# Down projection of a SwiGLU layer: where the gate and the residual are applied, and which engine adds the groups' sums

## The chip, the cores and the metric

The kernel runs on one core of a Trainium2 chip. The metric is the device time of one execution in microseconds. Engines are named as in the profile: PE is TensorE (matmul; PEld its weight load), DVE is VectorE, ACT is ScalarE, POOL is GpSimd, SP is the sync engine, whose queue issues the DMAs here.

## The reference

One inference step of a layer with 2048 features and 640 tokens (512 of the sample, 128 of the prompt): modulation, a mixer of attention and a recurrent scan, an output projection with residual and layer norm, then a SwiGLU layer with residual and a second layer norm. The change lies in the SwiGLU's last product and what stands behind it:

```python
def _post_norm(x, gate, f, g, b):
    return _layer_norm(ALPHA * x + gate * f, g, b)

def _swiglu(h, p):
    return (jax.nn.silu(h @ p["w_ffn_gate"]) * (h @ p["w_ffn_up"])) @ p["w_ffn_down"]

...
    x = _post_norm(x, g2, _swiglu(x * (1 + sc2) + sh2, p), p["ln2_g"], p["ln2_b"])
```

All inputs and outputs are float32. The gate g2 is one number per feature, another for the sample's tokens than for the prompt's. The kernel divides the whole by ALPHA, which the norm allows.

## The kernel before

Features lie on the 128 partitions, tokens along the free axis, in two halves `H1` and `H2` of 320 (the second half holds 192 tokens of the sample and 128 of the prompt). A float32 product is made of three products of float32r parts: weights are split into `qh` (cast on ACT) and `ql` (remainder, subtracted on DVE), operands likewise into a part and a remainder (tiles `p`, `t`).

The down projection has 22 pairs of contraction tiles in four groups c = 0 to 3 of 4, 6, 6 and 6 pairs. For each group, `operands` loads the pairs from `h_d` (tiles `hd`), forms Winograd's sums of them (POOL) and splits them (ACT casts, DVE remainders): per pair four POOL additions and, on DVE, one remainder `p` of 320 columns, one `p` of 640 and two `t` of 640. Then 8 pairs of feature tiles j follow, each one call of `strassen`: seven products in the order 1, 7, 5, 6, 2, 3, 4, each into a PSUM bank `b`. This is a set below. Sums of weights are formed on POOL and DVE (tiles `raw`). `strassen` copies product 1 to SBUF (`u1`, ACT), forms `u2` and `u3` on DVE and hands each of the four blocks of the result to `out(m, n, ps, u)`, as a bank and an SBUF tile to be added. In group c=3 products 2 and 4 are left out at first (the blocks of the first half of the tokens then have no bank, only `u1` and `u3`), and `rest` makes them behind all eight sets, so that the second half's norm can begin.

`out` is `gated`: DVE adds bank and tile to a tile `c` (L226), and multiplies by the gate and adds to the running result `z1` (L235), one instruction for a block of the first half and two, of 192 and 128 columns, for one of the second. `z1` begins as the residual: in group c=0 each of its 16 tiles is loaded from `z_d` (L1617) and gets the first norm's affine part on ACT (L238).

In c=3, `norms[1].add` takes each finished tile into the running sums of the layer norm, `nd` and `ns` on DVE, `nq` on ACT, `ns` on POOL. Behind the last group come the norms' ends and the output.

The order of each engine's instructions is set by a scheduler from the program's dependences and the tile pools' rooms: 8 small buffers of 320 columns (tag "ev": `c`, `u1` to `u3`, `nd`, `nq`), a pool of 640-column slots for `hd`, `p`, `t` and `z`, a few slots for weights. Each engine, SP's DMA queue too, then works in order.

Of the kernel before, what the change touches and what calls it, by code (L numbers as in the profile page):

```python
# [27 lines left out]
C = 64  # L28
# [40 lines left out]
# how long (us) the operands of a job's next products should take, beside the input projection and beside the attention  # L69
# [26 lines left out]
class Tensor:  # L96
    """TensorE, with a clock of the columns it has been given (us)"""
# [26 lines left out]
class Jobs:  # L124
    """The order of TensorE's work: of the jobs (generators) that are ready, the one of lowest rank goes on. A job yields the
    time until its next operands should be there, or a job to wait for"""
# [31 lines left out]
def step_kernel(ctx: ExitStack, tc: tile.TileContext, a: dict, o: dict, upto: int = 99, npairs: int = NPAIR, dbg=None):  # L158
# [81 lines left out]
    # ---- derived per-feature vectors  # L240
# [12 lines left out]
    # ---- weights: load, split in two float32r parts  # L253
# [19 lines left out]
    def mm3(ps, w, cols, x, first, last):  # L273
        """ps[128, 2, 0:320] += w.T @ x, both in two float32r parts"""
        (wh, wl), (xh, xl) = w, x
        for i, (ww, xx) in enumerate(((wh, xh), (wh, xl), (wl, xh))):
            for h in range(2):
                T.matmul(ps[:, h, :HN], ww[:, cols: cols + P], xx[:, h * HN: h * HN + HN],
                         start=first and i == 0, stop=last and i == 2)
            yield 0.0  # L280
# [6 lines left out]
    class Weights:  # L287
        """granules [128, 4 * 128] of weights in the order of use, each loaded and split while the one before is used"""
# [13 lines left out]
    def big(ps, ws, xs):  # L302
        """one feature tile"""
# [16 lines left out]
    # ---- adaLN  # L320
# [3 lines left out]
    def wmod_first(n, c0, w):  # L324
        """w columns from c0 on, in the room of what comes later"""
# [16 lines left out]
    def wmod_chunk(n, raws, c0=0, w=512):  # L342
        # in each group of 32 columns, the first two count
# [35 lines left out]
    # ---- input projection  # L379
# [22 lines left out]
    def token_shift(p0, p1, mi, mk=edge):  # L402
        """the tile's tokens (in two halves) shifted and mixed: 512 columns, one to skip, 128 columns"""
# [16 lines left out]
    # while w_mod streams in: the first feature tiles, two of them summed in PSUM, the others in SBUF  # L420
# [25 lines left out]
    def low_rank():  # L446
        """the decay's and the learning rate's low-rank inputs: leading parts twice along the partitions, remainders below
        each other"""
# [67 lines left out]
    def squares(j, t):  # L516
        """sums of squares of the queries' (4 tiles) and the keys' and values' (2 tiles) low-rank input, by token"""
# [13 lines left out]
    # ---- RWKV-7 heads, two at a time  # L531
# [9 lines left out]
    def hrow(h):  # L541
        """where head h keeps what pairs with its own features along the contraction"""
        return rows(1 - h)

    def wide(name):
        """[128, 10 chunks, 2, 64] in two slots' worth of memory"""
# [10 lines left out]
    def inverse(mab):  # L557
        """U = (I - N)^-1 for the strictly upper N of each chunk and head. Diagonal blocks of 16 in DVE's lanes, a block
        to a partition: (head, half) by (chunk of 16, block of 2), by substitution for 8 and one doubling; then two
        doublings on TensorE. Only the part of mab above the diagonal is used"""  # L560
# [18 lines left out]
        # the two blocks of 8 together  # L579
# [65 lines left out]
    def stat_cols(sq, rhs, n, bank=mps):  # L645
        """per 128 tokens: sum over the partitions of sq against rhs [128, n]; [128 tok, 5 * n] in PSUM"""
# [5 lines left out]
    def spread(st, n, ps2=None):  # L652
        """[128 tok, 5 * n] to [128, 640] feature-major, each of n columns on 128/n partitions: two PSUM tiles"""
# [22 lines left out]
    def nat(d, j):  # L676
        """tokens of half j of direction d, in natural order (read backward for d = 1)"""
# [7 lines left out]
    def rwkv_load(i):  # L685
        sh = {"carry": rtile("cy", 2 * C, "cy", 1)}
        raw = load_raw(a["lora"][i])
        # [leading parts; remainders] for the decay, [remainders; leading parts] for the learning rate
# [22 lines left out]
    def rwkv_decays(i, j, sh):  # L711
        """of the chunks of half j, in the order in which each direction reads them: decays within the chunk, keys"""
# [1213 lines left out]
```

## Time and profile before

| | |
|---|---|
| three runs | 3610.99, 3615.95, 3622.03 us; median 3615.95 |
| profiled execution, span | 3610.9 us |
| PE / DVE / ACT / POOL busy | 94% / 73% / 40% / 27% |
| down projection's first products | about 2934 us |
| c=1, c=2, c=3 begin | about 3057, 3230, 3405 us |

The stages ahead of the down projection take the first 2930 us. The profiled execution is one execution; its times are read against its own span. The starts of the groups are found by counting matmuls (672, 1008, 1008 and 1008 per group).

### The profile page before, as it was taken

The page shows a single profiled execution, that of the slowest core. Times are in us where ns is not written, and L with a number is a line of the kernel's source. Part 1 is how long each engine was busy: PE and PEld are TensorE (multiplying, and loading weights), DVE is VectorE, ACT ScalarE, POOL GpSimd, SP SyncE. Part 2 cuts the span into 40 slices and gives each one's busy share as a digit, 9 for nine tenths or more (in the row PEclk, how much of TensorE's full clock was granted, in tenths as well). Part 3 has the DMA queues.
Part 4 walks back from the last instruction along what each step waited for, and adds up shares of the span by engine and source line. Part 5 has one row for each costly group of instructions (what it writes and reads, how often), then busy time and mean ns, then how long its engine had stood idle before and what let it go on. Part 6 is the DMA issues. An engine that isn't in the chain of part 4 may idle for free. (4 is left out here: it accounts for less than half of the span.)

```text
span 3610.9 us, 70535 instructions
## 1 busy us (share of the span) xinstructions
PE 3388.5 (94%) x27538; PEld 3030.8 (84%) x27538; DVE 2625.3 (73%) x4729; ACT 1445.9 (40%) x2947; POOL 981.6 (27%) x944
## 2 busy tenths in 40 slices
PE   8979999999998999999979999999999988989887
PEld 4667777777886778799979999999999988989786
DVE  1455766676667777536998777777777799898998
ACT  1143433333343444423553444334444354444434
POOL 0021111120111222101374323333323353242545
PEclk9988999999998999999989999999999999999898
DMA  8653444444112111167534333333333343332333
GB/s 296 231 173 127 147 146 138 155 149 131 59 57 87 33 42 39 33 188 243 152 105 141 91 106 100 97 105 98 93 104 102 112 174 94 88 101 86 102 104 109
DMA packets 243054, 427.53 MB, mean 118 GB/s; under 512 B 25824, under 2 KB 76448, under 8 KB 242720
## 3 DMA queue, kind: packets, MB, share of 16 engines
q1 hardware_dynamic: 242720, 423.02, 37.1%
q8 instruction: 216, 3.54, 0.4%
q14 instruction: 118, 0.97, 0.1%
HBM read 374.73 MB, written 46.56 MB: 117 GB/s over the span
## 5 line engine op out<-in xcount | busy, mean ns | idle before, releaser
L226 DVE TENSOR_TENSOR ql<-raw,qh 128x512 fp32r<-128x512 f32 (+1 forms) x1072 | 870.7, 822 | 283.2 <-ACT qh L1325 277.0
L1325 ACT CAST qh<-raw 128x512 fp32r<-128x512 f32 (+1 forms) x1072 | 623.9, 586 | 928.9 <-PE b L112 782.9
L112 PE MATMUL b<-t,qh 128*128 128x320 f32 x4224 | 946.4, 313 | 18.2 <-ACT qh L1325 10.9
L112 PEld LDWEIGHTS b<-t,qh 128*128 128x128 f32 x4224 | 718.1, 191 | 23.5 <-ACT qh L1325 14.6
L112 PE MATMUL b<-p,qh 128*128 128x320 f32 x3168 | 713.0, 313 | 4.8 <-ACT qh L1325 3.3
L112 PE MATMUL b<-t,ql 128*128 128x320 f32 x2112 | 657.9, 315 | 32.3 <-DVE ql L226 32.0
L226 POOL TENSOR_TENSOR raw<-raw,raw 128x512 f32<-128x512 f32 (+1 forms) x288 | 390.4, 1357 | 862.4 <-DVE ql L226 664.7
L112 PEld LDWEIGHTS b<-p,qh 128*128 128x128 f32 x3168 | 538.5, 191 | 7.6 <-ACT qh L1325 5.2
L112 PE MATMUL b<-p,ql 128*128 128x320 f32 x1584 | 499.2, 315 | 36.1 <-DVE ql L226 35.7
L112 PEld LDWEIGHTS b<-t,ql 128*128 128x128 f32 x2112 | 401.8, 191 | 41.9 <-DVE ql L226 41.4
L112 PEld LDWEIGHTS b<-p,ql 128*128 128x128 f32 x1584 | 302.5, 191 | 45.7 <-DVE ql L226 45.6
L112 PE MATMUL acc<-xh,whi 128*128 128x320 f32 x1184 | 296.6, 333 | 6.2 <-ACT xh L269 5.9
L112 PE MATMUL acc<-xl,whi 128*128 128x320 f32 x1184 | 294.5, 331 | 0.0
L112 PE MATMUL acc<-xh,wlo 128*128 128x320 f32 x1184 | 292.6, 329 | 0.8 <-DVE wlo L226 0.8
L263 ACT CAST whi<-raw 128x512 fp32r<-128x512 f32 (+1 forms) x188 | 114.7, 610 | 340.1 <-PE acc L112 251.5
L226 DVE TENSOR_TENSOR wlo<-raw,whi 128x512 fp32r<-128x512 f32 (+1 forms) x188 | 129.3, 688 | 145.9 <-ACT whi L263 110.3
L112 PEld LDWEIGHTS acc<-xh,whi 128*128 128x128 f32 x1184 | 200.9, 195 | 34.4 <-issue 15.8
L226 DVE TENSOR_TENSOR raw<-raw,raw 128x512 f32<-128x512 f32 (+1 forms) x288 | 220.4, 777 | 8.8 <-POOL raw L226 6.3
L112 PEld LDWEIGHTS acc<-xh,wlo 128*128 128x128 f32 x1184 | 200.8, 195 | 22.2 <-issue 13.8
L112 PEld LDWEIGHTS acc<-xl,whi 128*128 128x128 f32 x1184 | 201.2, 195 | 19.3 <-issue 10.7
L112 PE MATMUL x<-wm,cs 128*32 128x512 f32 x768 | 140.3, 646 | 18.7 <-DMA wm<-in_w_mod_dram 18.2
L226 POOL TENSOR_TENSOR s<-s,c 128x320 f32<-128x320 f32 x88 | 104.6, 1189 | 138.6 <-DVE c L226 138.6
(329 smaller groups left out, 5134.4 us busy)
## 6 DMA issues: line engine op xcount, KB each, us to landing
wm<-in_w_mod_dram SPq DMA_DIRECT2D x64, 1024.0 KB, 5.4
raw<-in_w_gate_dram SPq DMA_DIRECT2D x188, 256.0 KB, 2.7
raw<-in_w_up_dram SPq DMA_DIRECT2D x188, 256.0 KB, 2.8
raw<-in_w_down_dram SPq DMA_DIRECT2D x224, 192.0 KB, 2.4
raw<-in_w_in_dram SPq DMA_DIRECT2D x132, 256.0 KB, 2.7
wm<-in_w_mod_dram SPq DMA_DIRECT2D x64, 512.0 KB, 6.2
raw<-in_w_out_dram SPq DMA_DIRECT2D x96, 256.0 KB, 3.1
hd<-s SPq DMA_DIRECT2D x44, 320.0 KB, 2.9
```

The source lines that it names most:

```text
L112: self.eng.matmul(out, lhsT, rhs, start=start, stop=stop)
L226: eng.tensor_tensor(out=out, in0=x, in1=y, op=op)
L263: A.copy(hi, r)
L1325: A.copy(hi, x)
```

## The change

For c < 3, `out` becomes `summed`: the blocks are added up without the gate. In c=0 DVE writes bank plus tile straight to `z1`, whose 16 tiles are now only rooms, taken ahead of the loop. In c=1 and c=2 POOL adds the SBUF tile to `z1`, then DVE adds the bank. For c=3, `gated` does the same POOL addition, DVE adds the bank if there is one, and then DVE multiplies by the gate and adds the residual. The residual is loaded there, per block of 320 columns, into a small buffer `zr` of the "ev" pool (`residual`, with the ACT instruction for the affine part). `rest` multiplies its bank by the gate and adds to `z1`, as before.

In numbers: 144 gate instructions on DVE go (six in each of 24 sets of c=0 to 2); 96 POOL additions of 128x320 come (64 in c=1 and 2, 32 in c=3); 16 loads of 320 KB and 16 ACT instructions on 640 columns in c=0 go, 32 loads of 160 KB and 32 ACT instructions on 320 columns in c=3 come. The products are the same. The rest of the diff removes comments.

```diff
-    def gated(kind, f, zz):
-        """z += gate * C"""
+    def summed(zz, first):
         def out(m, n, ps, u):
-            c = u if ps is None else ps if u is None else tmp("c")
-            if c is not ps and c is not u:
-                tt(V, c, ps, u, ALU.add)
+            z = zz[m][:, (H1, H2)[n]]
+            if first:
+                tt(V, z, ps, u, ALU.add)
+            else:
+                tt(G, z, z, u, ALU.add)
+                tt(V, z, ps, z, ALU.add)
+        return out
+    def gated(kind, f, zz, res):
+        def out(m, n, ps, u):
+            if u is not None:
+                z = zz[m][:, (H1, H2)[n]]
+                tt(G, z, z, u, ALU.add)
+                r = res(f + m, n)
+                if ps is not None:
+                    tt(V, z, ps, z, ALU.add)
             for o_, w, cnd in ((0, 192, 0), (192, 128, 1)) if n else ((0, HN, 0),):
                 z = zz[m][:, n * HN + o_: n * HN + o_ + w]
-                stt(z, c[:, o_: o_ + w], mcol(kind, f + m, cnd), z, ALU.mult, ALU.add)
+                g = mcol(kind, f + m, cnd)
+                if u is None:
+                    stt(z, ps[:, o_: o_ + w], g, z, ALU.mult, ALU.add)
+                else:
+                    stt(z, z, g, r[:, o_: o_ + w], ALU.mult, ALU.add)
         return out
...
-    # with the last of the contraction tiles, the second half of the tokens first
-    z1 = []
+    def residual(f, n):
+        r = tmp("zr")
+        DMA.dma_start(out=r, in_=z_d[f][:, (H1, H2)[n]])
+        act(r, r, AF.Identity, bias=vcol("ln1b", f), scale=vcol("ln1g", f))
+        return r
+    z1 = [fslot("z") for _ in range(KT)]
     k0 = 0
     for c, (npr, ng) in enumerate(((4, 1), (6, 2), (6, 2), (6, 2))):
         ops = operands(npr, lambda i: [loaded(h_d[2 * (k0 + i) + m], "hd") for m in range(2)], G)
         k0 += npr
         for j in range(8):
-            if c == 0:
-                for f in (2 * j, 2 * j + 1):
-                    z1.append(loaded(z_d[f], "z"))
-                    act(z1[f], z1[f], AF.Identity, bias=vcol("ln1b", f), scale=vcol("ln1g", f))
-            strassen(qs, ops, ng, gated(5, 2 * j, z1[2 * j: 2 * j + 2]), whole=c < 3)
+            zz = z1[2 * j: 2 * j + 2]
+            strassen(qs, ops, ng, summed(zz, c == 0) if c < 3 else gated(5, 2 * j, zz, residual), whole=c < 3)
             if c == 3 and j:
                 for z in z1[2 * j: 2 * j + 2] if j > 1 else z1[:4]:
                     norms[1].add(z)
...
             order = ExitStack()
             order.enter_context(tc.manual_schedule(engines={mybir.EngineType.PE}))
             for j in range(8):
-                rest(qs, ops, ng, gated(5, 2 * j, z1[2 * j: 2 * j + 2]))
+                rest(qs, ops, ng, gated(5, 2 * j, z1[2 * j: 2 * j + 2], None))
```

The first place is SP's queue while c=0 runs: `hd_5958` and the tiles behind it (before) and `hd_5926` and those behind it (after) are the operands of c=1's first pairs, `in_w_down4` are the weights of c=0, `in_w_down` those of c=1. Before:

```order
L1617 DMA z_5920_33430<-zd15_18068 128x640
L1617 DMA hd_5958_33593<-hd8_18017 128x640
L1617 DMA hd_5959_33595<-hd9_18018 128x640
L1387 DMA raw_5751_32659<-in_w_down4_dram 128x512
L1617 DMA hd_5960_33597<-hd10_18019 128x640
L1617 DMA hd_5961_33599<-hd11_18020 128x640
L1387 DMA raw_5755_32679<-in_w_down4_dram 128x512
L1387 DMA raw_5759_32698<-in_w_down4_dram 128x512
L1387 DMA raw_5766_32726<-in_w_down4_dram 128x512
L1617 DMA hd_5965_33610<-hd12_18021 128x640
```

After:

```order
L1387 DMA raw_5883_33273<-in_w_down4_dram 128x512
L1387 DMA raw_5898_33352<-in_w_down_dram 128x384
L1387 DMA raw_5899_33354<-in_w_down_dram 128x384
L1387 DMA raw_5903_33374<-in_w_down_dram 128x384
L1387 DMA raw_5904_33376<-in_w_down_dram 128x384
L1387 DMA raw_5908_33395<-in_w_down_dram 128x384
L1387 DMA raw_5909_33397<-in_w_down_dram 128x384
L1387 DMA raw_5915_33422<-in_w_down_dram 128x384
L1387 DMA raw_5916_33424<-in_w_down_dram 128x384
L1635 DMA hd_5926_33481<-hd8_18017 128x640
L1635 DMA hd_5927_33483<-hd9_18018 128x640
L1635 DMA hd_5928_33485<-hd10_18019 128x640
```

c=1's operands stood behind the residual's loads, among c=0's first weights; they now stand behind the last weights of c=0 and the first eight of c=1.

The second place is DVE, where the first of these operands are split. Before, this is the first third of c=0:

```order
L235 SCALAR_TENSOR_TENSOR z_5709_32473<-c_5734_32585,mod_90,z_5709_32473 128x320
L226 TENSOR_TENSOR p1_5962_33601<-hd_5958_33593,p1_5962_33601 128x320
L226 TENSOR_TENSOR c_5743_32629<-b_5740_32611,u3_5728_32558 128x320
L226 TENSOR_TENSOR ql_5742_32614<-raw_5716_32500,qh_5741_32613 128x512
L235 SCALAR_TENSOR_TENSOR z_5709_32473<-c_5739_32607,mod_90,z_5709_32473 128x192
L235 SCALAR_TENSOR_TENSOR z_5709_32473<-c_5739_32607,mod_90,z_5709_32473 128x128
L226 TENSOR_TENSOR p2_5964_33603<-hd_5959_33595,p2_5963_33602 128x640
L226 TENSOR_TENSOR ql_5748_32641<-raw_5720_32520,qh_5747_32640 128x512
L226 TENSOR_TENSOR ql_5753_32662<-raw_5724_32539,qh_5752_32661 128x512
L235 SCALAR_TENSOR_TENSOR z_5710_32476<-c_5743_32629,mod_90,z_5710_32476 128x320
```

After, it is c=0's end (`z_5653` is the last feature tile, `b_5922` its last product):

```order
L226 TENSOR_TENSOR z_5653_32237<-b_5922_33461,u3_5913_33416 128x320
L226 TENSOR_TENSOR ql_5983_33623<-raw_5981_33620,qh_5982_33622 128x384
L226 TENSOR_TENSOR p2_5932_33491<-hd_5927_33483,p2_5931_33490 128x640
L226 TENSOR_TENSOR p1_5935_33502<-hd_5928_33485,p1_5935_33502 128x320
L226 TENSOR_TENSOR p2_5937_33504<-hd_5929_33487,p2_5936_33503 128x640
L226 TENSOR_TENSOR t1_5939_33512<-hd_5926_33481,t1_5938_33511 128x640
L226 TENSOR_TENSOR t2_5941_33514<-hd_5927_33483,t2_5940_33513 128x640
L226 TENSOR_TENSOR p1_5944_33525<-hd_5933_33498,p1_5944_33525 128x320
L226 TENSOR_TENSOR p2_5946_33527<-hd_5934_33500,p2_5945_33526 128x640
L226 TENSOR_TENSOR t1_5948_33535<-hd_5928_33485,t1_5947_33534 128x640
L226 TENSOR_TENSOR ql_5985_33637<-raw_5898_33352,qh_5984_33636 128x384
L226 TENSOR_TENSOR t2_5950_33537<-hd_5929_33487,t2_5949_33536 128x640
```

The preparation of c=1's pairs was spread between additions, gate instructions and `ql` of c=0; it now stands nearly in a row between c=0's last addition and c=1's products, and the gate instructions are gone.

The third place is POOL in c=3, about one set; `raw` are sums of weights for later products, `ns1` the norm's running sum. Before:

```order
L226 TENSOR_TENSOR ns1_5636_32220<-ns1_5636_32220,nd_7037_38156 128x320
L226 TENSOR_TENSOR raw_7084_38353<-raw_7057_38246,raw_7055_38240 128x384
L226 TENSOR_TENSOR raw_7063_38275<-raw_7063_38275,raw_7056_38244 128x384
L226 TENSOR_TENSOR raw_7064_38277<-raw_7064_38277,raw_7057_38246 128x384
L226 TENSOR_TENSOR raw_7119_38511<-raw_7100_38434,raw_7098_38428 128x384
L226 TENSOR_TENSOR ns1_5636_32220<-ns1_5636_32220,nd_7079_38340 128x320
L226 TENSOR_TENSOR raw_7128_38543<-raw_7101_38436,raw_7099_38430 128x384
L226 TENSOR_TENSOR ns1_5636_32220<-ns1_5636_32220,nd_7081_38346 128x320
```

After:

```order
L226 TENSOR_TENSOR z_5640_32224<-z_5640_32224,u1_6904_37797 128x320
L226 TENSOR_TENSOR z_5638_32222<-z_5638_32222,u2_6886_37709 128x320
L226 TENSOR_TENSOR raw_6936_37937<-raw_6915_37849,raw_6913_37843 128x384
L226 TENSOR_TENSOR raw_6948_37983<-raw_6916_37851,raw_6914_37845 128x384
L226 TENSOR_TENSOR raw_6922_37880<-raw_6922_37880,raw_6915_37849 128x384
L226 TENSOR_TENSOR z_5641_32225<-z_5641_32225,u3_6929_37902 128x320 x2
L226 TENSOR_TENSOR raw_6923_37882<-raw_6923_37882,raw_6916_37851 128x384
L226 TENSOR_TENSOR z_5640_32224<-z_5640_32224,u2_6928_37901 128x320
L226 TENSOR_TENSOR ns1_5636_32220<-ns1_5636_32220,nd_6941_37964 128x320
L226 TENSOR_TENSOR raw_6985_38152<-raw_6964_38064,raw_6962_38058 128x384
```

The set of `z_5640` and `z_5641` has four such additions (three lines, one of them twice) among the sums of weights, each fed by a tile `u` of the current set; `z_5638` belongs to the set before.

## Rows read from the trace of the kernel before

**Rows 1.** The page's totals: engine, busy us (share of the span), x instructions.

```profile
PE 3388.5 (94%) x27538; PEld 3030.8 (84%) x27538; DVE 2625.3 (73%) x4729; ACT 1445.9 (40%) x2947; POOL 981.6 (27%) x944
```

**Rows 2.** By stretch: busy us (x) of each engine, PE clock, DMA share, GB/s.

```profile
2950.00:3080.00 130.00, 114.03 (x694) 106.91 (x693) 123.57 (x206) 51.22 (x96) 57.01 (x44) 0.92 0.30 91
3080.00:3180.00 100.00, 100.00 (x684) 100.00 (x683) 85.88 (x169) 40.72 (x81) 24.98 (x23) 1.00 0.30 88
3180.00:3240.00 60.00, 46.47 (x247) 42.83 (x246) 58.25 (x83) 27.75 (x53) 35.00 (x31) 0.86 0.39 117
...
3360.00:3410.00 50.00, 33.33 (x157) 28.88 (x156) 47.81 (x59) 20.23 (x37) 32.87 (x29) 0.80 0.33 101
3410.00:3530.00 120.00, 110.19 (x710) 105.53 (x709) 116.47 (x224) 48.37 (x102) 51.91 (x40) 0.99 0.37 106
```

**Rows 3.** Waits (total us, times, longest): 3183–3235, then two of 3410–3530.

```profile
PEld b L112 <- DVE ql L226: 12.1, 9, 3.7
...
PEld b L112 <- DVE ql L226: 14.3, 18, 1.9
...
DVE raw L226 <- POOL raw L226: 2.7, 3, 0.9
```

**Rows 4.** DVE forms, 2950–3080: x count | busy us, mean ns | idle.

```profile
L235 DVE SCALAR_TENSOR_TENSOR z<-c,mod,z 128x192 f32<-128x192 f32 x15 | 11.2, 744 | 0.0
...
L235 DVE SCALAR_TENSOR_TENSOR z<-c,mod,z 128x320 f32<-128x320 f32 x16 | 10.0, 628 | 0.0
...
L235 DVE SCALAR_TENSOR_TENSOR z<-c,mod,z 128x128 f32<-128x128 f32 x16 | 7.1, 447 | 0.0
```

**Rows 5.** DVE forms, 3180–3240, the turn from c=1 to c=2.

```profile
L226 DVE TENSOR_TENSOR c<-b,u 128x320 f32<-128x320 f32 x8 | 3.8, 479 | 0.0
L235 DVE SCALAR_TENSOR_TENSOR z<-c,mod,z 128x320 f32<-128x320 f32 x3 | 3.3, 1101 | 0.0
...
L235 DVE SCALAR_TENSOR_TENSOR z<-c,mod,z 128x128 f32<-128x128 f32 x3 | 1.6, 546 | 0.0
L235 DVE SCALAR_TENSOR_TENSOR z<-c,mod,z 128x192 f32<-128x192 f32 x3 | 1.2, 408 | 0.0
```

**Rows 6.** DVE in order of time, 3183–3215: start, us, line, form.

```profile
3187.55 1.16 DVE L226 TENSOR_TENSOR p<-hd,p 128x320 fp32r<-128x320 f32 x1
...
3207.86 0.48 DVE L226 TENSOR_TENSOR c<-b,u 128x320 f32<-128x320 f32 x1
3208.26 0.48 DVE L226 TENSOR_TENSOR u<-b,u 128x320 f32<-128x320 f32 x1
...
3214.79 0.48 DVE L226 TENSOR_TENSOR p<-hd,p 128x320 fp32r<-128x320 f32 x1
```

**Rows 7.** 3410–3530: DVE and POOL forms, then DVE's min/median/max ns.

```profile
L226 DVE TENSOR_TENSOR ql<-raw,qh 128x384 fp32r<-128x384 f32 x79 | 51.6, 667 | 1.9 <-ACT qh L1325 1.8
L226 DVE TENSOR_TENSOR raw<-raw,raw 128x384 f32<-128x384 f32 x28 | 19.3, 708 | 2.8 <-POOL raw L226 2.7
...
L226 DVE TENSOR_TENSOR ns<-ns,nq 128x320 f32<-128x320 f32 x13 | 9.8, 754 | 0.0
...
L226 POOL TENSOR_TENSOR raw<-raw,raw 128x384 f32<-128x384 f32 x27 | 36.4, 1351 | 51.6 <-DVE raw L226 28.4 <-DVE ql L226 23.2
L226 POOL TENSOR_TENSOR ns<-ns,nd 128x320 f32<-128x320 f32 x13 | 16.0, 1231 | 9.2 <-DVE nd L226 9.1
...
L226 DVE TENSOR_TENSOR ql<-raw,qh x79: 543/548/1364, 3410.7 to 3529.9; 128x384 fp32r<-128x384 f32 x79
...
L226 DVE TENSOR_TENSOR raw<-raw,raw x28: 543/547/1381, 3413.2 to 3512.6; 128x384 f32<-128x384 f32 x28
...
L226 DVE TENSOR_TENSOR ns<-ns,nq x13: 479/491/1303, 3436.5 to 3520.3; 128x320 f32<-128x320 f32 x13
```

**Rows 8.** ACT forms, 2890–3056: the residual's affine part.

```profile
L238 ACT ACTIVATE z<-z,vec 128x640 f32<-128x640 f32 x16 | 14.0, 917 | 0.0
```

## The prediction

> **What bounds the kernel now.** I read the page's totals first, then busy time by stretches of the down projection, then the waits inside three stretches, then DVE by form of instruction, and last single DVE instructions beside POOL's. TensorE is busy 94% of the span, DVE 73% [rows 1]. That average says nothing of the down projection. There the stretch 3080–3180, inside group c=1, shows what TensorE does when nothing holds it: 684 matmuls in 100 us, 6.84 per us, DVE at 86% [rows 2]. Every other stretch is held against that rate. 2950–3080 (most of c=0 and the turn to c=1): 694 matmuls need 101.5 us and took 130, so 28.5 are lost. 3180–3240 (turn to c=2): 247 need 36.1 of 60, 23.9 lost. 3360–3410 (turn to c=3): 157 need 23.0 of 50, 27.0 lost. 3410–3530 (c=3): 710 need 103.8 of 120, 16.2 lost. In all four DVE is busy 95 to 97% of the time [rows 2], and TensorE's weight loads wait longest for DVE's remainders `ql`: 12.1 us in 3183–3235, 14.3 us in 3410–3530 [rows 3]. So the projection has two regimes: TensorE bounds the middle of c=1 and c=2, DVE bounds c=0, the turns and c=3. A DVE microsecond is worth something only in the second.
>
> One property of DVE decides the sign. Its additions with one operand in PSUM take 0.48 us, and two such rows start 0.40 apart, so each overlaps the next by 0.08. The operand remainder `p<-hd,p`, whose inputs both lie in SBUF, took 0.48 us at 3214.79 and 1.16 us at 3187.55, while POOL was adding: 0.68 more [rows 6]. POOL's additions thus cost DVE time, though they run on another engine.
>
> **The change, part by part.**
>
> *Middle of c=1 and c=2.* Each Strassen product set loses six gate instructions on DVE and gains four POOL additions. TensorE bounds there, so both lie beside it: 0. The cover is the 14% of DVE that is idle in 3080–3180 [rows 2]; four stretches of 0.68 [rows 6] are 2.7 us per set, against six gate instructions taken away, so it doesn't vanish.
>
> *c=0 and the turn to c=1 (A).* Two things change. The gate instructions go: in 2950–3080 they are 11.2 + 10.0 + 7.1 = 28.3 us in 47 instructions [rows 4], less 47 × 0.08 overlap, 24.5 us. And the order moves: before, c=1's operands are loaded behind the 16 residual loads and three of their six pairs are prepared between c=0's products; after, those loads stand on SP behind all of c=0's weights and c=1's first ones, and on DVE the preparation of six pairs stands almost in a row. So DVE's relief falls in the middle of c=0, where TensorE then takes over as the bound, and the turn becomes one like c=1 to c=2, which loses 23.9 us. A = 23.9 − 28.5 = −4.6. Bounds: the whole relief comes back, −24.5; or the turn is like the worst one, 27.0 − 28.5 = −1.5. I take −4.6, because in the new order the preparation stands behind c=0's last sums, as it stands behind c=1's at that turn, with DVE 97% busy and POOL at 35 of 60 us [rows 2].
>
> *The three turns (B).* Each loses the gate instructions in it: 3.3 + 1.6 + 1.2 = 6.1 us in nine, less 9 × 0.08, 5.4 us [rows 5]. Eight additions `c<-b,u` stand in 3180–3240 [rows 5]; each now has a POOL addition in front of it, and some six of these fall where DVE is full. At 0.43 each (worked out below) that is 2.6, at 0.68 it is 4.1. I take a value between, 3.2, since the turns are where POOL is busiest: 35.0 of 60 us [rows 2]. B = 3 × (3.2 − 5.4) = −6.6, with ends at 3 × −5.4 = −16.2 and, were each POOL addition to cost its whole 1.23 us [rows 7], 3 × (7.4 − 5.4) = +6.0.
>
> *c=3 (C).* DVE's own list keeps its length: per set two additions and six gate instructions, before and after. What is new is 32 POOL additions of 128x320. What POOL costs DVE here today is read from the forms: `ql` 79 × (667 − 548) = 9.4 us, `raw` 28 × (708 − 547) = 4.5, `ns` 13 × (754 − 491) = 3.4, mean less median, together 17.3 us for POOL's 40 instructions, 0.43 each [rows 7]. 32 × 0.43 = 13.9 us. DVE is idle 120 − 116.5 = 3.5 us of the stretch [rows 2], which I let it hide: C = +10.4. Bounds: 0 if all of it falls beside PSUM operands, and 32 × 0.68 − 3.5 = +18.3.
>
> *New waits in c=3 (W).* DVE's additions now wait for POOL's; POOL waits for ACT's `u1` or DVE's `u3`, in order, and queued behind those waiting additions on POOL are sums `raw` that ACT's casts and then TensorE need. Today DVE waited for POOL's `raw` three times, 0.9 us at the longest [rows 3]. POOL goes from 51.9 busy of 120 us [rows 2] to 51.9 + 32 × 1.23 = 91, 76%. One such wait in every second of the eight sets: W = +4 (3.6); bounds 0 and two in every set, 14.4.
>
> *Residual.* 16 loads and 16 ACT instructions of 0.92 us [rows 8] leave c=0; half-size ones, 32 in number, come into c=3. Were each as long as a whole one, ACT would have 48.4 + 29.3 = 78 of 120 us there [rows 2]; DMA works at 0.37 of its share [rows 2]. Both stay beside DVE: 0. What they would cost without that cover stands under W, since DVE's gate instruction waits for ACT.
>
> TensorE's work and all stages ahead of the projection are as before: 0.
>
> **Sum.** −4.6 − 6.6 + 10.4 + 4 = +3.2 us. The profiled execution spans 3610.9 us, the lowest of the three runs (3610.99) and 5 us, 0.14%, under their median; I put the sum on the median: 3615.95 + 3.2 = **3619 us**. A measurement of this kernel can tell about 0.3% (10.8 us) from no change, so this forecast is "the same".
>
> **Rivals.**
>
> *1. The relief counts in full.* If the preparation of c=1's operands finds room on the relieved DVE, A is −24.5, and the first turn keeps only its POOL additions, +3.2: −24.5 + 3.2 − 4.4 + 10.4 = −15.3, 3601 us. For it: DVE is the bound in 2950–3080 at 95%. Against it: the new order doesn't let the preparation start before c=0 is nearly over. It decides if TensorE's rate stays at 6.84 until c=1's first products.
>
> *2. POOL becomes the pace of c=3, slower.* At 76% and in order, with 0.68 for each addition and two 0.9 us waits per set: A −4.6, B 3 × (4.1 − 5.4) = −3.9, C +18.3, W +14.4, together +24.2, 3640 us. For it: TensorE's and ACT's next weights are in the same POOL queue behind additions that wait for the set's sixth product. Against it: mean stretch today is 0.43, and POOL's sums run a set ahead. It decides once DVE waits for POOL in every set for longer than one DVE instruction.
>
> *3. A POOL addition costs DVE its whole length.* Today 17.3 us of stretch stand against 36.4 + 16.0 = 52.4 us of POOL [rows 7], a third, so the rows speak against it. If the new additions cost all of their 1.23: C = 39.4 − 3.5 = +35.9, B = +6.0, A −4.6, together +37, 3653 us. The Trainium skill (SBUF — State Buffer, Who interferes with whom) states this rule: a DVE instruction with two SBUF inputs and a POOL (GpSimd) instruction that reads SBUF exclude each other for the whole instruction, and one with a PSUM input isn't touched. The trace agrees in the second half (0.48 throughout) and, on the mean, shows a third of the first.
>
> *4. The stretch hides.* If C and W are 0, A and B alone give −11.2, 3605 us. For it: 3.5 us of idle DVE and TensorE's own work in c=3; against it: DVE is at 97% there.
>
> **How the numbers follow.** Forecast 0.46, alone from 3607 to 3630 (W from 0 to 14.4 on one side, B and C to their better halves on the other); rival 1 0.20, rival 2 0.20, rival 3 0.05, rival 4 0.09. Faster by over 0.3%: 0.16 of rival 1, 0.05 of rival 4, 0.04 of the forecast: 0.25. Slower: 0.18 of rival 2, 0.05 of rival 3, 0.09 of the forecast: 0.32. Within: 0.43. The range takes in rivals 1, 2 and 4 with a margin for the first, and leaves out rival 3 and the far ends: 3596 to 3642.
>
> **What would show it.** A: matmuls in c=0's first seven sets at 6.84 per us, then a turn that loses 20 to 25 us with DVE full. B: turns that lose 2 us less than before. C: in c=3 `ql` and `ns` with means 0.1 to 0.2 us above today's, POOL near 75%. W: a line "DVE waits for POOL" of 3 to 5 us. Wrong would be: c=0's turn without loss (rival 1), or TensorE in c=3 waiting for casts that wait for POOL (rival 2).

## The result, and the profile after

The changed kernel takes 3632.74 us (median of four runs, 3631.18 to 3635.67) against 3616.9 us for the kernel before, run beside it: a ratio of 1.0039, 95% interval 1.0027 to 1.0051, slower by 0.3 to 0.5%. 3619 was forecast, in a range of 3596 to 3642.

The page's totals (answering [rows 1]) show only that POOL works 109 us more and DVE 5 us less:

```profile
span 3630.3 us, 70534 instructions
...
PE 3399.2 (94%) x27538; PEld 3038.2 (84%) x27538; DVE 2620.5 (72%) x4585; ACT 1451.9 (40%) x2963; POOL 1090.4 (30%) x1040
```

The same stretches as in [rows 2], in the same columns (busy us and instructions of PE, PEld, DVE, ACT, POOL; then PE clock, DMA share, GB/s):

```profile
2950.00:3080.00 130.00, 114.78 (x697) 108.15 (x696) 107.16 (x160) 53.13 (x96) 57.40 (x47) 0.89 0.34 103
3080.00:3180.00 100.00, 100.00 (x684) 100.00 (x683) 83.02 (x136) 40.67 (x81) 49.65 (x46) 1.00 0.30 89
3180.00:3240.00 60.00, 45.83 (x252) 41.81 (x251) 57.76 (x71) 28.26 (x54) 47.59 (x38) 0.86 0.36 112
...
3360.00:3410.00 50.00, 36.26 (x179) 32.02 (x178) 49.41 (x52) 21.77 (x40) 43.73 (x35) 0.83 0.34 103
3410.00:3530.00 120.00, 96.32 (x606) 88.71 (x605) 118.91 (x189) 53.50 (x111) 73.97 (x65) 1.00 0.42 126
```

TensorE's count in 3410–3530 fell from 710 to 606, with DVE as busy as ever and POOL at 74.0 us instead of 51.9. At the stretch around the turn to c=1 the counts are alike (697 and 694), though DVE is busy 16 us less.

Counts in fixed stretches mix the groups, so from here on each set is timed by a landmark: ACT copies the set's first product (`u<-b`) once per set, 32 times in the projection, and from one copy to the next is a set's length. I write c.j for group and set. (These copies also set right the starts of the groups in the table ahead of the prediction: in the kernel before they stand at 2927.4, 3050.4, 3226.1 and 3398.3 us for 0.0, 1.0, 2.0 and 3.0, where the table has about 2934, 3057, 3230 and 3405.) ACT's copies in order of time (start, us, form, idle time before it), first of the kernel before, sets 0.0, 0.2, 0.4, 0.7 and 1.2:

```profile
2927.39 0.40 ACT L1477 COPY u<-b 128x320 f32<-128x320 f32 x1
...
2952.13 0.42 ACT L1477 COPY u<-b 128x320 f32<-128x320 f32 x1
...
2988.34 0.43 ACT L1477 COPY u<-b 128x320 f32<-128x320 f32 x1 [3.33 <-PE b L112]
...
3026.67 0.43 ACT L1477 COPY u<-b 128x320 f32<-128x320 f32 x1
...
3092.66 0.42 ACT L1477 COPY u<-b 128x320 f32<-128x320 f32 x1
```

and of the changed kernel, sets 0.0, 0.7 and 1.2:

```profile
2928.17 0.42 ACT L1477 COPY u<-b 128x320 f32<-128x320 f32 x1
...
3015.38 0.42 ACT L1477 COPY u<-b 128x320 f32<-128x320 f32 x1
...
3093.74 0.42 ACT L1477 COPY u<-b 128x320 f32<-128x320 f32 x1
```

From 0.0 to 0.7 is 99.3 us before and 87.2 after, seven sets of 12.3 each but the first: TensorE's own pace. Before, sets 0.2 and 0.3 alone took 36.2 us, 11.6 over that pace; the other five took 12.1 to 12.8 each, gate instructions and all. In those two sets stood 8 of the 24 remainders `p` and `t` of c=1's operands, and DVE was busy without a gap (36.27 of the 36.3 us from 2952 to 2988.3). From 0.7 to 1.2 is 66.0 before and 78.4 after. All lengths so read, us:

| stretch | before | after | after less before |
|---|---|---|---|
| c=0, sets 0.0 to 0.7 | 99.3 | 87.2 | −12.1 |
| turn, 0.7 to 1.2 | 66.0 | 78.4 | +12.4 |
| c=1, 1.2 to 1.7 | 92.4 | 92.1 | −0.3 |
| turn, 1.7 to 2.2 | 80.3 | 79.8 | −0.5 |
| c=2, 2.2 to 2.7 | 92.4 | 92.4 | 0 |
| turn, 2.7 to 3.1 | 59.1 | 56.2 | −2.9 |
| c=3, 3.1 to 3.7 | 103.1 | 122.2 | +19.1 |
| 3.7 to the end | 90.9 | 93.8 | +2.9 |
| first copy to the end | 683.5 | 702.1 | +18.6 |

The two profiled executions differ by 19.4 us (the copies begin 0.8 later), the medians by 15.8. The first copy lies between 2927 and 2936 us in the kernels below, whose code ahead of it is the same; so a kernel's profile is read by these lengths, and its time by its ratio. Each length comes from one profiled execution. Some repeat closely where the code is alike: the turn 0.7 to 1.2 is 78.4 in the six kernels below that keep it as it is. Others don't: c=0 takes 85.9 to 88.6 us in those six, by its first set, and c=3 in its changed form 122.2 in the changed kernel, but 118.7 and 119.5 in e5 and e9, which leave c=3's code alone. A difference of 3 us in those two stretches therefore settles nothing. The sums of lengths stray from the ratios by up to 4.5 us (for the changed kernel 18.6 against 0.39%, 14.1).

Where c=0's gain goes is seen on SP and DVE. SP's queue in the changed kernel (start, us it took to issue, form, count):

```profile
3000.38 17.60 SPq L1387 DMA_DIRECT2D raw<-in_w_down_dram  x8
3018.07 1.81 SPq L1635 DMA_DIRECT2D hd<-hd  x4
```

The first weights of c=1 keep SP for 17.6 us: SP's own waits from 2995 to 3060 are 37.0 us for DVE's `ql`, which frees their rooms. The operands' loads are issued only at 3018.07; in the kernel before the first was issued at 2938.6. DVE then gets the preparation in one piece (in order of time):

```profile
3026.68 0.48 DVE L226 TENSOR_TENSOR p<-hd,p 128x320 fp32r<-128x320 f32 x1
...
3028.49 3.29 DVE L226 TENSOR_TENSOR p<-hd,p 128x640 fp32r<-128x640 f32 x3
3031.70 1.48 DVE L226 TENSOR_TENSOR t<-hd,t 128x640 fp32r<-128x640 f32 x1
3034.69 0.82 DVE L226 TENSOR_TENSOR t<-hd,t 128x640 fp32r<-128x640 f32 x1 [1.51 <-ACT t L1325]
3035.43 2.56 DVE L226 TENSOR_TENSOR p<-hd,p 128x320 fp32r<-128x320 f32 x2
3037.92 1.49 DVE L226 TENSOR_TENSOR t<-hd,t 128x640 fp32r<-128x640 f32 x1
3039.33 1.22 DVE L226 TENSOR_TENSOR ql<-raw,qh 128x384 fp32r<-128x384 f32 x1
```

All 24 remainders `p` and `t` stand in this turn, where the kernel before had 16, and most are stretched: three `p` in 3.29 us, one `t` in 1.48 and another in 0.82. Between 3028 and 3040 there is one `ql` for TensorE. The turn as a whole, 0.7 to 1.2, before and after, in the columns of [rows 2]:

```profile
3027.00:3093.00 66.00, 56.70 (x344) 53.76 (x343) 62.38 (x108) 28.98 (x57) 31.09 (x25) 0.90 0.31 95
...
3015.00:3094.00 79.00, 63.78 (x350) 57.15 (x349) 72.73 (x94) 34.35 (x66) 53.29 (x45) 0.83 0.35 110
```

DVE is idle for 3.6 us of the turn before and for 6.3 after, and TensorE's granted clock is 0.90 before and 0.83 after. In the changed kernel it is 0.50 from 3030 to 3054, the lower of TensorE's two levels (1.2 GHz), after TensorE had been busy for 0.70 us of the four from 3026 to 3030.

c=3, sets 3.1 to 3.7 (3414 to 3536), DVE by form, as in [rows 7]:

```profile
L226 DVE TENSOR_TENSOR ql<-raw,qh 128x384 fp32r<-128x384 f32 x69 | 48.5, 721 | 0.0
L226 DVE TENSOR_TENSOR raw<-raw,raw 128x384 f32<-128x384 f32 x25 | 21.5, 873 | 1.1 <-DMA raw<-in_w_down_dram 1.1
L226 DVE TENSOR_TENSOR ns<-ns,nq 128x320 f32<-128x320 f32 x11 | 10.3, 938 | 0.0
L235 DVE SCALAR_TENSOR_TENSOR z<-z,mod,zr 128x128 f32<-128x128 f32 x14 | 9.8, 702 | 0.0
...
L226 DVE TENSOR_TENSOR z<-b,z 128x320 f32<-128x320 f32 x14 | 6.7, 477 | 0.0
```

POOL in the same stretch:

```profile
L226 POOL TENSOR_TENSOR raw<-raw,raw 128x384 f32<-128x384 f32 x26 | 33.3, 1282 | 32.7 <-DVE ql L226 20.1 <-DVE raw L226 12.6
L226 POOL TENSOR_TENSOR z<-z,u 128x320 f32<-128x320 f32 x27 | 30.2, 1134 | 7.9 <-DVE u L226 7.4
```

and two of its waits (total us, times, longest):

```profile
PEld b L112 <- DVE ql L226: 28.8, 25, 3.0
...
DVE raw L226 <- DMA raw<-in_w_down_dram: 1.1, 1, 1.1
```

`ql` went from a mean of 667 to 721 ns, `raw` from 708 to 873, `ns` from 754 to 938, and the 128-column gate instruction, of which the shortest takes 334, to 702; in the kernel before, from 3410 to 3530, it stood at 343:

```profile
L235 DVE SCALAR_TENSOR_TENSOR z<-c,mod,z 128x128 f32<-128x128 f32 x16 | 5.5, 343 | 0.0
```

The additions with a PSUM operand stayed where they were (477 ns, `c<-b,u` before 479 [rows 5]). In this stretch of the changed kernel DVE was never waiting for POOL, only for one load: it was busy 120.9 of 122 us with 195 instructions.

### The profile page after: what moved, and what is told of

It reads as the page before. It is cut to its first block, busy times and chain, and to the rows that moved or that the text cites. A ratio compares the mean times of both kernels' runs of the same rounds, so it can differ in the third digit from the quotient of the medians.

```text
span 3630.3 us, 70534 instructions
## 1 busy us (share of the span) xinstructions
PE 3399.2 (94%) x27538; PEld 3038.2 (84%) x27538; DVE 2620.5 (72%) x4585; ACT 1451.9 (40%) x2963; POOL 1090.4 (30%) x1040
## 4 chain that ended last, share of the span: by engine, by line
PE 59%; DVE 10%; issue 3%; ACT 2%; DMA 2%; POOL 1%; SPq 0%; DVEq 0%; ACTq 0%; POOLq 0%
PE b L112 41%; PE acc L112 10%; PE m L112 6%; DVE ql L226 2%; DVE z L226 1%; PE x L112 1%; DVE t L226 1%; DVE raw L226 1%; POOL z L226 1%; DVE z L235 1%; DVE p L226 1%; PE acc L116 0%; DMA raw<-in_w_down_dram 0%; POOL hd L226 0%; DVE ns L226 0%
## 5 line engine op out<-in xcount | busy, mean ns | idle before, releaser
L226 DVE TENSOR_TENSOR ql<-raw,qh 128x512 fp32r<-128x512 f32 (+1 forms) x1072 | 906.2, 855 | 302.7 <-ACT qh L1325 283.6
L112 PE MATMUL b<-t,qh 128*128 128x320 f32 x4224 | 949.4, 313 | 19.2 <-ACT qh L1325 11.0
L112 PEld LDWEIGHTS b<-t,qh 128*128 128x128 f32 x4224 | 718.8, 191 | 25.1 <-ACT qh L1325 13.5
L112 PE MATMUL b<-p,ql 128*128 128x320 f32 x1584 | 499.2, 316 | 24.1 <-DVE ql L226 23.9
L112 PEld LDWEIGHTS b<-t,ql 128*128 128x128 f32 x2112 | 401.9, 191 | 56.3 <-DVE ql L226 55.8
L112 PEld LDWEIGHTS acc<-xh,wlo 128*128 128x128 f32 x1184 | 201.2, 195 | 21.2 <-issue 12.8
L112 PEld LDWEIGHTS acc<-xl,whi 128*128 128x128 f32 x1184 | 201.8, 196 | 20.0 <-issue 10.6
L112 PE MATMUL x<-wm,cs 128*32 128x512 f32 x768 | 139.9, 641 | 18.2 <-DMA wm<-in_w_mod_dram 17.4
```

Of the source, the lines that this page charges most:

```text
L112: self.eng.matmul(out, lhsT, rhs, start=start, stop=stop)
L226: eng.tensor_tensor(out=out, in0=x, in1=y, op=op)
```

## The experiments

Theory S: what c=3 loses, it loses because POOL's additions stretch DVE's instructions with two SBUF operands, and DVE has no gap there. Theory R: it is the residual's loads and ACT instructions. Theory Q: it is the new waits, in line on POOL, ACT and DVE. Theory P: c=0's gain is real, and lost again because the order puts all of c=1's preparation into the turn. Lengths of all runs, us, read as above, and the ratio to the kernel before run beside each (interval):

| kernel | c=0 | turn | c=1 | turn | c=2 | turn | c=3 | end | sum | ratio |
|---|---|---|---|---|---|---|---|---|---|---|
| before | 99.3 | 66.0 | 92.4 | 80.3 | 92.4 | 59.1 | 103.1 | 90.9 | 683.5 | 1 |
| after | 87.2 | 78.4 | 92.1 | 79.8 | 92.4 | 56.2 | 122.2 | 93.8 | 702.1 | 1.0039 (1.0027–1.0051) |
| e1_c3_without | 87.4 | 78.4 | 92.1 | 79.8 | 92.4 | 56.3 | 102.2 | 92.3 | 681.1 | 0.9983 (0.9969–0.9997) |
| e2_c3_narrow | 88.6 | 78.4 | 92.1 | 80.9 | 92.4 | 55.4 | 106.0 | 91.4 | 685.3 | 0.9993 (0.9980–1.0006) |
| e3_c3_aside | 86.1 | 78.4 | 92.1 | 79.8 | 92.4 | 56.5 | 118.6 | 93.4 | 697.3 | 1.0033 (1.0021–1.0045) |
| e4_gate_c2 | 87.3 | 78.4 | 92.1 | 84.6 | 95.9 | 61.0 | 103.1 | 91.2 | 693.6 | 1.0024 (1.0012–1.0036) |
| e5_ahead | 91.8 | 70.2 | 92.1 | 79.2 | 92.1 | 57.4 | 118.7 | 93.6 | 695.2 | 1.0029 (1.0015–1.0043) |
| e7_c3_dve | 85.9 | 78.4 | 92.1 | 79.8 | 92.4 | 57.1 | 114.9 | 92.5 | 693.2 | 1.0026 (1.0015–1.0037) |
| e8_spread | 90.7 | 70.7 | 93.8 | 84.4 | 94.3 | 60.1 | 102.4 | 91.2 | 687.7 | 1.0011 (1.0001–1.0020) |
| e9_turns_narrow | 87.4 | 76.8 | 92.5 | 73.7 | 92.5 | 54.0 | 119.5 | 93.6 | 689.9 | 1.0013 (1.0002–1.0024) |
| e10_before_c0_plain | 93.1 | 61.9 | 92.4 | 80.1 | 92.4 | 57.5 | 104.2 | 91.3 | 672.9 | 0.9973 (0.9962–0.9985) |
| e11_moved | 91.7 | 68.7 | 94.7 | 80.3 | 94.4 | 58.3 | 104.1 | 91.2 | 683.3 | 0.9994 (0.9985–1.0003) |

The times that the expectations name are on the scale of the first runs, with the kernel before at 3617; its median beside the experiments was 3620 to 3621, so ratios are compared.

### c=3: length or waits

**No addition on POOL in c=3.**

```diff
                 z = zz[m][:, (H1, H2)[n]]
-                tt(G, z, z, u, ALU.add)
                 r = res(f + m, n)
```

> Leaves out the 32 POOL additions of group c=3 (the blocks lack the sums' SBUF part); the residual's loads and ACT instructions stay. Theory S (POOL's additions stretch DVE, which is busy without a gap in c=3): the time from c=3's begin on falls back to before's, some 20 us under the changed kernel, about 3613 us, with ql's mean in c=3 back from 710 ns to about 670. Theory Q (new waits: DVE and ACT in line behind POOL's additions): the same 20 us, so this run alone doesn't part S from Q. Theory R (the residual's loads and ACT instructions are what c=3 pays for): no change, about 3632.

The ratio fell by 0.56%, 20 us. ACT's copies 3.1 and 3.7:

```profile
3417.44 0.41 ACT L1477 COPY u<-b 128x320 f32<-128x320 f32 x1
...
3519.66 0.40 ACT L1477 COPY u<-b 128x320 f32<-128x320 f32 x1
```

102.2 us, a little under the kernel before, with all of the residual's loads and ACT instructions in place: theory R is out, and the residual costs c=3 nothing that shows. DVE is busy 102.9 of the 103 us from 3417 to 3520, with 192 instructions, against 120.9 us for 195 in the changed kernel: nearly the whole loss lies in the length of DVE's instructions. The 128-column gate instruction of this run in c=3 (DVE by form):

```profile
L235 DVE SCALAR_TENSOR_TENSOR z<-z,mod,zr 128x128 f32<-128x128 f32 x14 | 5.4, 384 | 0.0
```

384 ns instead of 702. `ql`'s mean, however, stayed at 710 and didn't come down to 670, so one form's mean is no measure by itself.

**The additions on 16 columns.** The line becomes `tt(G, z[:, :16], z[:, :16], u[:, :16], ALU.add)`.

> The same 32 additions in c=3, on 16 of 320 columns each (the other columns lack the sums' SBUF part): every wait and every place in POOL's queue stays, only the length goes. Theory S: POOL holds DVE up only as long as it works, so nearly all of the 20 us come back: 3613 to 3618. Theory Q: the waits are as before, 3628 to 3633.

0.46% under the changed kernel, c=3 106.0 us. POOL by form, and ACT's copies 3.1 and 3.7:

```profile
L226 POOL TENSOR_TENSOR z<-z,u 128x16 f32<-128x16 f32 x27 | 13.0, 491 | 7.2 <-DVE u L226 7.2
```

```profile
3422.45 0.42 ACT L1477 COPY u<-b 128x320 f32<-128x320 f32 x1
...
3528.44 0.41 ACT L1477 COPY u<-b 128x320 f32<-128x320 f32 x1
```

16.2 of the 20.0 us that e1 gets back came back with every wait in place. Of the 106.0 us DVE is busy for 100.4, and it waits 5.6 us for POOL's `raw`: what is left against e1 is waiting. That is what theory S expects, but a shorter addition also shortens a wait for it, so this run alone doesn't rule out theory Q; the next does.

**The additions in full, into a tile that nobody reads.**

```diff
+        if c == 3:
+            aside = fslot("aside")[:, :HN]
+            G.memset(aside, 0.0)
...
-                tt(G, z, z, u, ALU.add)
+                tt(G, aside, aside, u, ALU.add)
```

> The 32 additions in c=3 in full width, but into a tile of their own that nobody reads (the blocks lack the sums' SBUF part): POOL works as long and reads SBUF as much, and DVE no longer waits for any of them. Theory S: as slow as the changed kernel, 3630 to 3634. Theory Q: 3613 to 3618.

As slow as the changed kernel within the intervals, c=3 118.6 us. POOL by form, and the copies:

```profile
L226 POOL TENSOR_TENSOR aside<-aside,u 128x320 f32<-128x320 f32 x27 | 29.0, 1074 | 3.8 <-DVE u L226 2.8
```

```profile
3421.59 0.42 ACT L1477 COPY u<-b 128x320 f32<-128x320 f32 x1
...
3540.19 0.41 ACT L1477 COPY u<-b 128x320 f32<-128x320 f32 x1
```

With nobody waiting for their results, the additions cost 118.6 − 102.2 = 16.4 us in this stretch, which holds 27 of the 32: 0.61 each. From 2.7 to the end, with all 32, e3 is 17.7 us longer than e1, 0.55 each, and by the ratios 0.50%, 18 us. DVE is busy 117.8 of the 118 us from 3422 to 3540, with 190 instructions, and waits for nothing but 0.2 us of ACT. Theory S holds, and theory Q is out as the main cause. The 3.6 us to the changed kernel's 122.2 are no more than c=3 with the same code differs by between kernels (118.7 in e5, 119.5 in e9).

**The additions on DVE.** `tt(V, z, z, u, ALU.add)` in the same place.

> The 32 additions of c=3 on DVE instead of POOL. Theory S: DVE, busy without a gap, pays 0.48 to 0.54 us less 0.08 overlap for each, 13 to 15 us, and saves the stretch of 16 us and the waits of 4 us: some 5 us under the changed kernel, about 3628. Rival (DVE's stretch by POOL's sums of weights and of the norm grows with each further two-operand instruction): each addition costs 0.6 or more, no gain: 3632.

0.13% under the changed kernel, with intervals that overlap, so the runs show no gain; by lengths c=3 falls from 122.2 to 114.9 and the sum by 8.9, in a profiled execution (3624.1 us) that is quicker than the median of this kernel's runs (3631.7). DVE by form, the new additions:

```profile
L226 DVE TENSOR_TENSOR z<-z,u 128x320 f32<-128x320 f32 x27 | 15.2, 581 | 0.0
```

581 ns each, less the overlap of 0.08: 13.5 us for the 27 in this stretch, of which 114.9 − 102.2 = 12.7 us, 0.47 each, show in its length; from 2.7 to the end 13.7 us for 32, 0.43 each. By the ratios (e7 less e1, 0.43%) it is 0.49, against 0.57 for POOL's additions in e3, and the intervals of e3 and e7 overlap. This agrees with theory S; and DVE has little room there for work of any kind.

### c=0 and the turns

**The change's part in c=0 alone, on the kernel before.**

```diff
+    def plain(zz):
+        def out(m, n, ps, u):
+            tt(V, zz[m][:, (H1, H2)[n]], ps, u, ALU.add)
+        return out
...
-            strassen(qs, ops, ng, gated(5, 2 * j, z1[2 * j: 2 * j + 2]), whole=c < 3)
+            strassen(qs, ops, ng, (gated(5, 2 * j, z1[2 * j: 2 * j + 2]) if c else plain(z1[2 * j: 2 * j + 2])), whole=c < 3)
```

> The kernel before with one part of the change alone: in c=0 the 48 gate instructions are left out (DVE writes bank plus tile to z, which loses residual and gate of that group); the residual's loads and ACT instructions stay in c=0, and c=1's operands are still loaded and three of their pairs begun early. Theory P (the change's own relief in c=0 is lost because the order moves the preparation into the turn): here the order stays, so the middle of c=0 falls from 99 us to 88 to 92 and the turn to c=1 keeps its 66 us: 8 to 11 us under the kernel before, about 0.3%. Rival (the relief can't be kept in any order, the turn takes it back): within 3 us of the kernel before.

0.27% faster than the kernel before. SP's loads of operands (duration ns min/median/max, first and last start), and ACT's copies 0.0, 0.7 and 1.2:

```profile
L1622 SPq DMA_DIRECT2D hd<-hd x16: 319/349/425, 2946.0 to 3055.8; - x16
```

```profile
2933.97 0.41 ACT L1477 COPY u<-b 128x320 f32<-128x320 f32 x1
...
3027.03 0.42 ACT L1477 COPY u<-b 128x320 f32<-128x320 f32 x1
...
3088.95 0.42 ACT L1477 COPY u<-b 128x320 f32<-128x320 f32 x1
```

The loads begin at 2946.0, the middle of c=0 is 6.2 us shorter than before and the turn isn't longer but 4.1 shorter. So the relief of the 48 gate instructions is worth 10 us, provided the preparation stays spread. Theory P. Set against the changed kernel, this run also prices the new order: from 93.1 and 61.9 to 87.2 and 78.4, c=0 gains 5.9 us more and the turn loses 16.5 (1.6 of it by POOL's additions, e9 below), 10.6 net.

**Preparation ahead, in the changed kernel.** `operands` becomes a generator that stops behind each pair's step; three steps of c=1's run within c=0:

```diff
+            if c == 0 and j in (1, 2, 3):
+                next(part)
             zz = z1[2 * j: 2 * j + 2]
```

> The changed kernel, with three steps of the preparation of c=1's operands written between c=0's second and fourth sets: three pairs are loaded there, and on DVE 6 of the 24 remainders move from the turn into the middle of c=0. Theory P (the gain of 12 us in the middle of c=0 is lost again because all preparation falls in the turn to c=1): the six remainders, 2 x (0.73 + 1.31 + 1.04) = 6 us by their means at the other turn, leave the turn, and the middle of c=0 has room for them: about 3627 us, 6 under the changed kernel. Rival: the turn loses time through c=0's last set, which is shorter than c=1's and covers less, or through late loads alone: no change from moving remainders beyond 2 us.

By runs −0.10%, which the intervals don't tell from nothing. By lengths the turn falls by 8.2 us, more than forecast, and c=0 grows by 4.6, which the expectation had at none: 3.6 us net. It agrees with theory P on where the turn's time comes from, and shows that the middle of c=0 isn't free.

**Narrow additions in c=1 and c=2.** `tt(G, z[:, :16], z[:, :16], u[:, :16], ALU.add)` in `summed`.

> The 64 POOL additions of c=1 and c=2 on 16 of 320 columns (the blocks lack the sums' SBUF part there). TensorE bounds the middles, so only the turns can move. Theory S at the turns: each of the three has five to eight such additions while DVE is full, 0.5 us each: 2 to 4 us per turn come back, about 3625 us. Rival (a turn's length is set by the chain of preparation, POOL and ACT with DVE, not by DVE's total): under 2 us in all, 3631 to 3633.

0.26% under the changed kernel. The turns fall by 1.6, 6.1 and 2.2 us, the middles not at all. So at the turn 1.7 to 2.2 the POOL additions had cost 6 us; as that turn came out 0.5 us shorter than before, the gate instructions must have given back about as much.

### Versions

**Gate and residual with c=2.** `summed` for c < 2, `gated` with the residual for c=2, and for c=3 `gated` as in the kernel before.

> Gate and residual one group earlier: c=0 and c=1 plain sums, c=2 with POOL addition, gate and residual, c=3 as in the kernel before (no POOL addition, gate and add). If c=3's POOL additions cost 20 us (S or Q) and TensorE bounds the middle of c=2 with room on DVE, the 20 us come back and the turn to c=3 gives back some 3: about 3615, the kernel before within 0.3%. If c=2's middle has no room for POOL additions and six gate instructions together, its sets of 84 us per 576 matmuls grow and the time stays over 3622.

c=3 is back at 103.1, but only 0.15% are gained, with intervals that overlap: c=2's sets take 19.2 us instead of 18.5 (95.9 for five), and the turns on either side of it lose 4.8 us each. Waits in c=2 (3253 to 3372):

```profile
POOL z L226 <- DVE raw L226: 22.7, 4, 5.7
...
DVE ql L226 <- ACT qh L1325: 13.3, 20, 1.8
...
PEld b L112 <- DVE ql L226: 7.5, 8, 2.2
```

POOL's additions wait for DVE's sums, and TensorE for `ql` again, in a stretch where it was busy throughout before (111 of 111 us, 3247 to 3358). DVE isn't full here as it is in c=3: it is busy 100.5 of 119 us, and its `ql` wait for ACT's casts. So c=2's loss isn't shown to be stretched DVE instructions; which of POOL's additions and the residual's ACT instructions holds up the casts wasn't tried. The second branch of the expectation.

**Half in c=1, half in c=2, with preparation ahead.** `gated` with the residual for j = 1, 3, 5, 6 in c=1 and 0, 2, 4, 7 in c=2.

> c=3 as in the kernel before, the preparation of three pairs ahead as in e5, and gate and residual in the middle groups, half of the pairs of feature tiles j in c=1 (1, 3, 5, 6), half in c=2 (0, 2, 4, 7), so that a heavy set (four POOL additions, six gate instructions) has light ones beside it. If TensorE still bounds those sets: 19 us back in c=3, 6 at the turn to c=1, less some 5 for the heavy sets at the turns: about 3613 us, faster than the kernel before by 0.1 to 0.2%. If heavy sets cost as much as in the version with all of them in c=2 (15 us): 3622.

The main expectation missed: 0.11% slower than the kernel before, 687.7 us by lengths, near the second branch. The middles grew by less than 2 us (93.8 and 94.3), the turns beside heavy sets by 4.6 and 3.9 (84.4 and 60.1).

**No POOL addition at a turn or in c=3.** In c=2 the pairs go in the order 2, 3, 7, 0, 1, 4, 5, 6; `gated` with the residual for 2 to 6 in c=1 and 7, 0, 1 in c=2; the plain additions of c=1 on DVE; c=3 as in the kernel before and the preparation of three pairs ahead, as in e5.

> A version built from the findings: c=0 plain with three steps of preparation ahead; in c=1 gate and residual for the pairs 2 to 6 in the middle, pairs 0, 1, 7 plain with additions on DVE; in c=2 the pairs in the order 2, 3, 7, 0, 1, 4, 5, 6, so that 7, 0 and 1 get gate and residual in its middle, the others add and gate as in the kernel before; c=3 as in the kernel before. No POOL addition stands at a turn or in c=3. By the lengths of the runs so far (c=0's middle and first turn 160 us, the middles 93.5 and 94, the turns 79.5 and 59, c=3 102.4) the projection takes 679 us against 683.5 of the kernel before: 4 us, 0.1% faster. If heavy sets in a row can't be hidden in the middles, 2 us more in each: no gain.

0.9994 (0.9985 to 1.0003): no gain that can be told. By lengths it is 4.3 us over the estimate of 679, 1.2 of it in c=1 and 1.7 in c=3, under 1 us in every other stretch. No version beat the kernel before beyond its interval, e1 and e10 aside, which leave work out.

## Why the prediction was right or wrong, point by point

The time fell within the range, but outside the likeliest case's own 3607 to 3630, and 0.4% slower is just beyond what that case called the same. It lies between the forecast and rival 2, and the range holds it by the room left for that rival, whose mechanism, DVE waiting for POOL, is not what happened. By lengths the forecast is 15.4 us short (18.6 against 3.2), 7.1 of it in A, 6.0 in C and 2.9 at the end.

**Bound by stretch: right for c=1, c=2 and c=3.** TensorE bounds the middles of c=1 and c=2; they moved by 0.3 us or less. In c=0 DVE was the bound only in the two sets where the preparation stood; the mean over 2950–3080 hid that.

**A, c=0 and its turn: forecast −4.6, with the first turn's share of B −6.8; measured +0.3.** The first half was right: c=0 went to TensorE's pace and gained 12.1. The step that failed is pricing its turn like the one to c=2, with 23.9 lost. At full pace 0.7 to 1.2 takes 12.3 + 2 × 18.5 = 49.3 us; it lost 16.7 before and 29.1 after, while the turn to c=2 lost 24.3 (79.8 − 3 × 18.5). The likeness fails further when POOL's additions are narrow (e9): they give back 1.6 us here and 6.1 there, which leaves 27.5 lost against 18.2. Against e10 the preparation put into a row costs the turn 16.5 us and saves c=0 only 5.9. Why this turn is so much worse than the one to c=2 is open. One reason argued is that c=0's last set covers less of the preparation: behind its first product 6/7 of 12.3 us remain, of c=1's last set 6/7 of 18.5, 5.3 us more. DVE's idle time (6.3 us here, 3.7 of 80 at the turn to c=2) and TensorE's granted clock (0.83 here, 0.89 there) may make up the rest; no run parts them. Rival 1 was right that the relief is worth 10 us (e10), and the forecast right that the new order forfeits it.

**B, the other two turns: forecast −2.2 each; measured −0.5 and −2.9.** The sum is near, its terms weren't: e9 puts POOL's additions at the turn to c=2 at 6.1 us against the 3.2 taken, about 0.5 us for each of the twelve in that turn and its two sets (the forecast counted six), and so, by difference, the gate instructions at 6.6 against 5.4. That the two errors partly cancel is luck.

**C, POOL's additions in c=3: forecast +10.4; measured +16.4 (e3 less e1).** The mechanism was right, the term too small in two places: 0.55 to 0.61 us each instead of 0.43 (some forms had been left out of that mean), and 3.5 us of idle DVE taken off as cover, which wasn't there: without the additions (e1) DVE is busy 102.9 of 103 us as well.

**W, waits: forecast +4; at most 1.1 on DVE,** and that for a load: the line "DVE waits for POOL" isn't there, DVE is busy 120.9 of 122 us. Rival 2's waits are out with it. (Such waits do stand in e2, 5.6 us, where DVE is less full.)

**Residual: forecast 0, right in c=3** (e1). **The end: forecast 0, measured +2.9,** of which e1 shows 1.4 without POOL's additions; the rest wasn't traced.

**Rival 3, the whole length of an addition:** e3's stretch has 16.4 us of cost for 29.0 us of POOL in its 27 additions. The rule of the Trainium skill (SBUF — State Buffer, Who interferes with whom) is exclusion for the whole instruction; read as a price that DVE alone pays, it would make 29. The trace shows a little over half. DVE's additions with a PSUM operand stayed untouched (476 to 482 ns in c=3 of every kernel read there), as that section of the Trainium skill states. The run doesn't contradict the exclusion itself: POOL's additions took 0.86 us at the shortest and 1.07 on the mean, so part of their time may be their own waiting, and part may lie beside DVE instructions that read PSUM; these parts weren't measured apart.

## What to carry to other kernels

An addition moved from VectorE to GpSimd isn't free where VectorE is full: here it cost some 0.55 us on the clock for each, and doing it on VectorE itself no more than that (0.43 to 0.49), so ask of each stretch which engine ends last before moving work between these two. A gain in a stretch can be lost at its end if the new order puts off the next stretch's preparation; look at the load queue's order, where it shows first: here the first load went from 2938.6 to 3018.1 us. Time sets by a landmark instruction rather than by totals: gains and losses of 12 us side by side show up only so.

## What was not expected of the hardware

A short DVE instruction pays as much for POOL's work as a long one. The gate instructions of c=3 on 128 and on 320 columns, beside additions on 16 columns (e2) and beside full ones (e3):

```profile
L235 DVE SCALAR_TENSOR_TENSOR z<-z,mod,zr 128x320 f32<-128x320 f32 x14 | 7.5, 538 | 0.0
...
L235 DVE SCALAR_TENSOR_TENSOR z<-z,mod,zr 128x128 f32<-128x128 f32 x14 | 4.7, 339 | 0.0
```

```profile
L235 DVE SCALAR_TENSOR_TENSOR z<-z,mod,zr 128x320 f32<-128x320 f32 x14 | 11.5, 851 | 0.0
...
L235 DVE SCALAR_TENSOR_TENSOR z<-z,mod,zr 128x128 f32<-128x128 f32 x14 | 9.0, 644 | 0.0
```

Both grew by about 310 ns. Which form pays depends on what it stands beside: in the kernel before the 128-column one took 343 ns in c=3, but 725 in the middle of c=1. POOL's instructions, too, are longer beside a full DVE. An addition of 16 columns took 491 ns in c=3 (e2), beside a full DVE, where the shortest took 217; in c=1 and c=2 (e9), where DVE has gaps, about half of the 64 took 222 or less.
